# Moving the high and low parts of x by 224 bytes inside a partition

## The chip, the cores and the metric

The kernel runs on one core of one Trainium2 chip. The metric is the device time of the whole program in microseconds, median of the runs; lower is better. The profile beside it is one execution of the same program, with the start and the length of every instruction on every engine.

## The reference

Two layers of a decoder trunk over 256 tokens of width 1024 in float32. Layer 0 mixes tokens with stick-breaking attention, layer 1 with block-sparse attention, which over 256 tokens is plain causal softmax attention with rotary positions; each is followed by a squared-ReLU MLP of width 4096, and each of the four sub-layers closes with a layer norm over a scaled residual.

```python
    h = x
    for i in range(DEPTH):            # DEPTH = 2
        ln1_g, ln1_b, w1, w2, ln2_g, ln2_b = channel[i]
        h = layer_norm(DEEPNORM_ALPHA * h + mixers[i % N_MIXERS](h), ln1_g, ln1_b)
        h = layer_norm(DEEPNORM_ALPHA * h + squared_relu_mlp(h, w1, w2), ln2_g, ln2_b)
    return h
```

## The kernel before

Every large matmul is made of three: a float32 operand is split into a high part (rounded by a copy on ScalarE, L203) and a low part (the rest, a subtraction on VectorE, L204), and the product is high times high, high times low and low times high, added up in PSUM. `mm` (L189) issues one of them, `mm3` (L191) the three. In a matmul one operand, the stationary one, is loaded into the array as a block of 128x128, and the other, the moving one, streams past it. The trace names them in the order out<-moving,stationary.

The weights arrive as 64 "units" a layer of 1 MB, 512 rows by 512 columns, through SyncE's DMA queue into three raw buffers; ScalarE and VectorE split each into a `hi` and a `lo` tile, of which five pairs are live. The activations of a sub-layer's input stand transposed in two tiles for the whole program, `xh` and `xl` (eight blocks of 128 rows by 256 tokens each). Five loops read these:

- `projT` computes a transposed product: the stationary operand is a block of `hi` or `lo`, the moving one a row of `xh` or `xl` with 256 columns. It makes the queries and keys of layer 0 (`qkT_ps`) and the first MLP product (`up_ps`) of chunks 2 to 7 of both layers: the rows `qkT_ps<-xh,hi` and `up_ps<-xh,hi` and their two sisters each.
- `proj` computes tokens by columns: the stationary operand is a block of `xh` or `xl` (128 tokens), the moving one a row of `hi` or `lo` with 512 columns. It makes the values (`v_ps`) of both layers, the queries and keys (`qk_ps`) of layer 1 and the first two MLP chunks (`up_ps<-hi,xh`, from `up_tok`) of both layers.
- `down` (`dn_ps`) and `wo` (`wo_ps`) have the same shape as `proj`, with 512 moving columns of `hi` or `lo`, but their stationary blocks come from the tiles `hh`, `hl` (the MLP's hidden layer) and `oh`, `ol` (the attention's output).
- the scores (`sc`) multiply blocks of `qkh` and `qkl`, two heads beside each other on 64 partitions each; `o` multiplies the weights of the attention (`pt` moving) with the values (`v` stationary).
- transposes on TensorE (`xt`, `ht_ps`, `tp`, `pt_ps`) move the identity out of `const` past a stationary block of `h`, `r`, `qk` or `p`.

The order of all instructions is written out when the program is built: `Plan` holds a clock for each engine, with a fixed cost for each operation by its size, and issues what is due. Its costs know nothing of addresses. A norm (`norm`) is followed by `to_x`, which transposes the new `h` on TensorE and writes `xh` and `xl` again; the next `proj` waits for them.

The tiles stand in a partition in the order in which their pools are opened, each rounded up to 32 bytes. Where they begin, in bytes of the partition and modulo 512 (every block, row and buffer of a kind is a multiple of 512 bytes away from the first, but for the ten `t2k` and four `t3k` buffers):

| tile | first byte | modulo 512 |
|---|---|---|
| xh, xl | 2176, 10368 | 128 |
| h (2), v (2) | 18560, 26752 | 128 |
| const (identity) | 36000 | 160 |
| raw (3), hi (5), lo (5) | 50080, 74656, 115616 | 416 |
| qkh, qkl, r, qk, rot (ten t2k buffers) | 156576 | 416, 448, 480, 0, 32, ... 192 |
| p, keep (four t3k buffers) | 177376 | 224, 256, 288, 320 |
| pt (4) | 189792 | 352 |
| hh, oh (3), hl, ol (3) | 202080, 214368 | 352 |

Of the kernel before, what the change touches and what calls it, by code (L numbers as in the profile page):

```python
# [7 lines left out]
F32 = mybir.dt.float32  # L8
# [6 lines left out]
P = 128  # L15
# [11 lines left out]
SEQ = (("A0", "V0", "A1", "A2", "A3", "V1"), ("A0", "A1", "V0", "A2", "A3", "V1"))  # L27

RAWS, LIVE = 3, 5
N2K, N3K, NPT = 10, 4, 4  # L30
MARGIN, WINDOW = 0.5, 0.25
X_LOADS = {0: 1, 1: 1, 2: 2, 4: 2, 6: 2}
# [121 lines left out]
def trunk(ctx: ExitStack, tc: tile.TileContext, x, xt, cst, cstb, w, ln, out):  # L154
    nc = tc.nc

    def pool(name, bufs, **kw):
        return ctx.enter_context(tc.tile_pool(name=name, bufs=bufs, **kw))

    one = pool("one", 1)  # L160
# [39 lines left out]
    def split(n, hi, lo, src, after, rank=1, take=(), give=(), scale=None):  # L200
# [9 lines left out]
        b.first = a  # L210
        return b

    xh = one.tile([P, KT, T], F32R, tag="xh", name="xh")
    xl = one.tile([P, KT, T], F32R, tag="xl", name="xl")
    h = [one.tile([P, D], F32, tag=f"h{t}", name=f"h{t}") for t in range(NT)]
    v = [one.tile([P, D], F32, tag=f"v{t}", name=f"v{t}") for t in range(NT)]

    def tok(t):
        return slice(t * P, (t + 1) * P)
# [561 lines left out]
```

## Time and profile before

| | us |
|---|---|
| median of 3 runs | 613.29 (612.9 to 613.78) |
| the profiled execution, its own time | 613.18 |
| its span, from the first to the last instruction | 611.4 |
| TensorE busy in the span | 600.0 |
| VectorE, ScalarE, GpSimd busy | 389.4, 290.6, 24.6 |

Matmuls overlap: a record lasts from when a matmul starts to when its last result is out, and the next one starts long before that. So the busy time of TensorE says only that it never rests; what a matmul costs is the distance from its start to the next start. The chain of work that ended last gives it: it merges stretches of matmuls of one kind and writes their count and their time.

### The profile page before, as it was taken

What the parts mean: (1) busy time and instruction counts of PE and PEld (TensorE: products, weight loads), DVE (VectorE), ACT (ScalarE), POOL (GpSimd) and SP (SyncE); (2) the same over time, 40 slices, a digit from 0 to 9 for tenths busy, and PEclk for the clock granted to TensorE, in tenths of its full rate; (3) what the DMA queues carried; (4) which work ended last, traced back from release to release, by engine and by line L of the source; (5) the groups of instructions that cost most, each with busy time, mean ns of one, the idle gap of its engine ahead of it and who ended that gap; (6) DMA issues with size and microseconds to landing.
All of it is one profiled execution on the core that took longest, in us unless ns stands there. A gap on an engine that the chain in (4) does not pass through costs nothing.

```text
span 611.4 us, 8761 instructions
## 1 busy us (share of the span) xinstructions
PE 600.0 (98%) x3640; PEld 513.7 (84%) x3640; DVE 389.4 (64%) x489; ACT 290.6 (48%) x419; POOL 24.6 (4%) x30
## 2 busy tenths in 40 slices
PE   8999999999999999999999999999999999999994
PEld 6899987878899899898877777778798998898883
DVE  5787774777546445545779777768666437437444
ACT  5676663436444443543535655635356326335310
POOL 0000000000000000000032022000000000000000
PEclk9999999999999999999999999999999999999998
DMA  8984236175556346337175333332664374364201
GB/s 283 383 304 181 99 140 244 51 252 184 199 209 232 143 177 258 147 146 274 70 214 199 139 138 137 138 139 96 248 254 162 141 270 154 148 249 190 87 0 69
DMA packets 17751, 109.31 MB, mean 179 GB/s; under 512 B 1968, under 2 KB 2352, under 8 KB 5680
## 3 DMA queue, kind: packets, MB, share of 16 engines
q1 hardware_dynamic: 17712, 108.76, 48.6%
q8 instruction: 28, 0.46, 0.3%
q14 instruction: 11, 0.09, 0.0%
HBM read 107.71 MB, written 1.05 MB: 178 GB/s over the span
## 4 chain that ended last, share of the span: by engine, by line
PE 95%; DVE 2%; DMA 1%; ACT 1%; SPq 0%; issue 0%; DVEq 0%; ACTq 0%
PE dn_ps L189 29%; PE up_ps L189 29%; PE wo_ps L189 7%; PE v_ps L189 7%; PE qkT_ps L189 7%; PE qk_ps L189 7%; PE sc L189 3%; PE o L496 2%; DMA raw<-in_wqkv 1%; PE xt L373 1%; PE tp L543 1%; DVE lo L204 1%; DVE xl L204 1%; PE ht_ps L650 1%; PE pt_ps L478 1%; PE pt_ps L480 1%
## 5 line engine op out<-in xcount | busy, mean ns | idle before, releaser
L204 DVE TENSOR_TENSOR lo<-raw,hi 128x1024 fp32r<-128x1024 f32 (+1 forms) x196 | 229.8, 1213 | 47.8 <-ACT hi L203 46.0
L203 ACT CAST hi<-raw 128x1024 fp32r<-128x1024 f32 (+1 forms) x196 | 192.0, 1032 | 63.3 <-issue 42.4
L189 PE MATMUL up_ps<-xh,hi 128*128 128x256 f32 x384 | 108.1, 281 | 0.0
L189 PE MATMUL up_ps<-xl,hi 128*128 128x256 f32 x384 | 107.9, 281 | 0.0
L189 PE MATMUL up_ps<-xh,lo 128*128 128x256 f32 x384 | 107.8, 281 | 0.0
L189 PE MATMUL dn_ps<-hi,hl 128*128 128x512 f32 x256 | 100.8, 394 | 0.0
L189 PE MATMUL dn_ps<-lo,hh 128*128 128x512 f32 x256 | 100.2, 391 | 0.0
L189 PE MATMUL dn_ps<-hi,hh 128*128 128x512 f32 x256 | 99.7, 390 | 0.0
L617 DVE SCALAR_TENSOR_TENSOR r<-up_ps,r 128x512 f32<-128x512 f32 x32 | 22.0, 688 | 83.4 <-ACT r L615 83.4
L189 PEld LDWEIGHTS up_ps<-xl,hi 128*128 128x128 f32 x384 | 72.4, 188 | 0.5
L189 PEld LDWEIGHTS up_ps<-xh,hi 128*128 128x128 f32 x384 | 72.3, 188 | 0.5
L189 PEld LDWEIGHTS up_ps<-xh,lo 128*128 128x128 f32 x384 | 72.3, 188 | 0.0
L615 ACT ACTIVATE r<-up_ps 128x512 f32<-128x512 f32 x32 | 19.1, 596 | 100.5 <-PE up_ps L189 100.5
L189 PEld LDWEIGHTS dn_ps<-lo,hh 128*128 128x128 f32 x256 | 48.1, 188 | 10.6
L189 PEld LDWEIGHTS dn_ps<-hi,hh 128*128 128x128 f32 x256 | 48.1, 188 | 10.0
L189 PEld LDWEIGHTS dn_ps<-hi,hl 128*128 128x128 f32 x256 | 48.1, 188 | 9.8
L189 PE MATMUL qkT_ps<-xh,hi 128*128 128x256 f32 x128 | 37.6, 294 | 1.3 <-ACT hi L203 1.3
L189 PE MATMUL qkT_ps<-xh,lo 128*128 128x256 f32 x128 | 36.6, 286 | 0.2 <-DVE lo L204 0.2
L189 PE MATMUL qkT_ps<-xl,hi 128*128 128x256 f32 x128 | 36.4, 285 | 0.0
L203 ACT CAST xh<-xt 128x512 fp32r<-128x512 f32 x12 | 7.0, 587 | 42.9 <-PE xt L373 41.1
L189 PEld LDWEIGHTS qkT_ps<-xh,hi 128*128 128x128 f32 x128 | 24.6, 192 | 2.6 <-ACT hi L203 2.1
L189 PE MATMUL v_ps<-hi,xh 128*128 128x512 f32 x64 | 26.6, 416 | 0.0
(97 smaller groups left out, 889.2 us busy)
## 6 DMA issues: line engine op xcount, KB each, us to landing
raw<-in_w SPq DMA_DIRECT2D x64, 1024.0 KB, 5.0
raw<-in_wqkv SPq DMA_DIRECT2D x22, 1024.0 KB, 5.9
raw<-in_wo SPq DMA_DIRECT2D x8, 1024.0 KB, 4.7
raw<-in_wqkv SPq DMA_DIRECT2D x8, 256.0 KB, 6.5
gb<-in_l_ln_g SPq DMA_DIRECT2D x4, 512.0 KB, 3.7
gb<-in_l_ln_b SPq DMA_DIRECT2D x4, 512.0 KB, 5.2
h<-in_x SPq DMA_DIRECT2D x2, 512.0 KB, 6.7
out<-h SPq DMA_DIRECT2D x4, 256.0 KB, 2.1
```

The source lines that it names most:

```text
L189: nc.tensor.matmul(ps, sta, mov, start=start, stop=stop)
L203: f = lambda: nc.scalar.copy(hi(), src())
L204: g = lambda: nc.vector.tensor_tensor(lo(), src(), hi().bitcast(F32), op=ALU.subtract)
L373: nc.tensor.transpose(XB[t][:, n, k * P:(k + 1) * P], h[t][:, (4 * n + k) * P:(4 * n + k + 1) * P], ident)
L478: nc.tensor.transpose(ps[:, j, 0:P], pj[:, T:T + P], ident)
L480: nc.tensor.transpose(ps[:, j, T:T + P], pj[:, P:T], ident)
L496: nc.tensor.matmul(o[HD * j:HD * j + HD, 0, kt * P:T], v[kt][:, hd * HD:(hd + 1) * HD], pt[:, 0:T] if kt == 0 else pt[:, T:T + P], start=k ...
L543: nc.tensor.transpose(tb["tp"][:, pr, c0:c0 + P], QK[g, t]["qk"][:, e * T + pr * P:e * T + pr * P + P], ident)
L615: nc.scalar.activation(box["r", n], ps, AF.Relu)
L617: return dve(512, lambda: nc.vector.scalar_tensor_tensor(box["r", n], ps, 0.0, box["r", n], op0=ALU.max, op1=ALU.mult), after=[a], rank=0. ...
L650: nc.tensor.transpose(box["ht"][:, 0, k * P:(k + 1) * P], box["r", 0][:, k * P:(k + 1) * P], ident)
```

## The change

Two tiles that nothing reads or writes are put into the pool `one`: 224 bytes ahead of `xh` and 288 bytes behind `v`. `xh`, `xl`, the two `h` and the two `v` begin 224 bytes later, at 352 modulo 512 instead of 128. Everything behind them begins 512 bytes later, so that it keeps its place modulo 512. No instruction is added, removed or moved.

```diff
+GAP = (224, 288)
...
+    def shift(n):
+        one.tile([P, n // 4], F32, tag=f"gap{n}", name=f"gap{n}")
+
+    shift(GAP[0])
     xh = one.tile([P, KT, T], F32R, tag="xh", name="xh")
     xl = one.tile([P, KT, T], F32R, tag="xl", name="xl")
     h = [one.tile([P, D], F32, tag=f"h{t}", name=f"h{t}") for t in range(NT)]
     v = [one.tile([P, D], F32, tag=f"v{t}", name=f"v{t}") for t in range(NT)]
+    shift(GAP[1])
```

## Rows read from the trace of the kernel before

**Rows 1.** Page: span; each engine's busy time, share of the span, instructions
```profile
span 611.4 us, 8761 instructions
...
PE 600.0 (98%) x3640; PEld 513.7 (84%) x3640; DVE 389.4 (64%) x489; ACT 290.6 (48%) x419; POOL 24.6 (4%) x30
```

**Rows 2.** Page: chain that ended last, shares by engine, then by line
```profile
PE 95%; DVE 2%; DMA 1%; ACT 1%; SPq 0%; issue 0%; DVEq 0%; ACTq 0%
PE dn_ps L189 29%; PE up_ps L189 29%; PE wo_ps L189 7%; PE v_ps L189 7%; PE qkT_ps L189 7%; PE qk_ps L189 7%; PE sc L189 3%; PE o L496 2%; DMA raw<-in_wqkv 1%; PE xt L373 1%; PE tp L543 1%; DVE lo L204 1%; DVE xl L204 1%; PE ht_ps L650 1%; PE pt_ps L478 1%; PE pt_ps L480 1%
```

**Rows 3.** Waits of TensorE: for whom, us in total, times, longest
```profile
PE qkT_ps L189 <- ACT hi L203: 1.3, 1, 1.3
...
PE o L496 <- ACT pt L485: 0.2, 1, 0.2
```

**Rows 4.** Windows: stretch, its length, busy us of engines (instructions), clock, DMA
```profile
150.00:296.00 146.00, 146.00 (x903) 131.29 (x902) 80.35 (x86) 60.96 (x74) 0.99 (x1) 1.00 0.52 194
303.00:394.00 91.00, 90.76 (x513) 70.05 (x511) 72.19 (x124) 49.37 (x106) 16.29 (x9) 1.00 0.50 172
```

**Rows 5.** Groups of TensorE by form: count, busy us, mean ns, idle before
```profile
L189 PE MATMUL up_ps<-xh,hi 128*128 128x256 f32 x384 | 108.1, 281 | 0.0
...
L189 PE MATMUL dn_ps<-hi,hl 128*128 128x512 f32 x256 | 100.8, 394 | 0.0
...
L189 PE MATMUL qkT_ps<-xh,hi 128*128 128x256 f32 x128 | 37.6, 294 | 1.3 <-ACT hi L203 1.3
...
L189 PE MATMUL v_ps<-hi,xh 128*128 128x512 f32 x64 | 26.6, 416 | 0.0
```

**Rows 6.** Chain in order of time: start, us, what, count; undisturbed stretches
```profile
157.59 10.99 PE dn_ps L189 x48
168.58 11.36 PE up_ps L189 x96
...
303.37 6.29 PE qk_ps L189 x27
...
421.99 6.29 PE up_ps L189 x27
...
570.63 32.98 PE dn_ps L189 x144
```

**Rows 7.** Timeline of TensorE: first and last of the matmuls with x stationary
```profile
19.52 0.39 PE L189 MATMUL v_ps<-hi,xh 128*128 128x512 f32 x1
...
446.71 0.39 PE L189 MATMUL up_ps<-hi,xl 128*128 128x512 f32 x1
```

**Rows 8.** Chain in order of time: from the norm to layer 1's products
```profile
309.66 0.44 PE xt L373 x4
310.10 0.69 PE qk_ps L189 x3
310.79 0.66 PE xt L373 x4
311.47 0.59 ACT xh L203
312.09 1.29 DVE xl L204 x2
313.38 1.14 DVE lo L204
314.57 11.23 PE qk_ps L189 x47
```

**Rows 9.** Timeline of TensorE: one block of transposes of p
```profile
71.58 0.27 PE L478 MATMUL pt_ps<-const,p 128*128 128x128 f32 x1
...
72.13 0.27 PE L480 MATMUL pt_ps<-const,p 128*128 128x128 f32 x1
```

**Rows 10.** Timeline of TensorE: pairs of score matmuls, two blocks of 16
```profile
48.40 0.28 PE L189 MATMUL sc<-qkl,qkh 64*128 64x256 f32 x2
...
48.63 0.23 PE L189 MATMUL sc<-qkh 64*128 64x128 f32 x2
...
329.13 0.28 PE L189 MATMUL sc<-qkl,qkh 64*128 64x256 f32 x2
...
329.37 0.22 PE L189 MATMUL sc<-qkh 64*128 64x128 f32 x2
```

## The prediction

> **What bounds the kernel now.** The page comes first: TensorE is busy for 600.0 of 611.4 us, VectorE for 389.4 and ScalarE for 290.6 [rows 1]. Busy time of overlapping matmuls proves little, so the chain comes second: 95% of it is TensorE [rows 2], and nearly all of that the three-part products of `mm`, two shares of 29% for the MLP and four of 7% for the attention's projections. The waits come third: TensorE waits hardly at all once the first weights are there, 1.3 us for the first of them and 0.2 us at a single later place [rows 3]. The windows by stage come last: in the MLP of layer 0, and in the stage of layer 1 in which x is the stationary operand of almost everything, the granted clock is 1.00, the level of 2.4 GHz, and VectorE, the next busiest, is busy for 72.19 of 91 us [rows 4]. So the time is the sum of the distances from one matmul's start to the next, in a fixed order. A change that alters this distance alters the time; one that leaves it alone doesn't.
>
> **What a start costs, by operand.** The chain's stretches give the distance. With 512 moving columns and a stationary block of `hh` or `hl` (at 352 modulo 512), 48 matmuls take 10.99 us, 229.0 ns each, and 144 take 32.98, again 229.0 [rows 6]. With the same moving tiles, the same 512 columns and a stationary block of x (at 128), 27 take 6.29 us, 233.0 ns each, in layer 1's queries and in the MLP alike [rows 6]. All these run at the one clock, each in a steady rhythm. Shape, type, moving operand and PSUM use agree between the two kinds; what differs is the tile that the stationary block is read from. Whichever of the three buffers of `hh`, or of the five of `hi`, is in use, the rhythm stays, so large distances in a partition don't seem to matter, and the place modulo 512 is the difference that is left. With 256 moving columns of x (at 128) and a stationary block of `hi` or `lo` (at 416), 96 take 11.36 us, 118.3 ns each [rows 6].
>
> **The change part by part.** It adds and removes no instruction, and as the plan's costs know no address, the order stays.
>
> (a) x as stationary operand of `proj`. Nine groups of 64 have it, like the one shown: three parts each in `v_ps`, `qk_ps` and `up_ps` [rows 5], 576 matmuls between 19.52 and 446.71 us [rows 7]. Between these two rows 512 of the 576 are followed by the next start after 224 to 245 ns; the other 64 stand ahead of other work or of a wait and keep what they cost. With x at 352 and the weights still at 416, both places modulo 512 are those of `down`. So 512 x (233.0 - 229.0) = 2.05 us are saved. If the other 64 gain as well it is 576 x 4.0 = 2.30 us.
>
> (b) Of that, something is given back. At three places (before the second MLP chunk of either layer, and in layer 1's queries, the one shown) TensorE waits behind a norm: the second transposes of `xt`, then 0.59 us of ScalarE, 1.29 and 1.14 us of VectorE, then the products go on [rows 8]. The matmuls ahead of the transposes lie on the chain, but the 12 between these and the wait lie beside it: what they gain lengthens the wait. That is 3 x 12 x 4.0 ns = 0.15 us. What is late next there is VectorE's `lo`, and it is no later than now. Elsewhere VectorE has room: 72.19 of 91 us [rows 4] against a stage that shrinks by some 1.2 us (about 300 starts of 4.0 ns).
>
> (c) x as moving operand of `projT`: 1536 matmuls, three groups of 384 in the MLP and three of 128 in layer 0's queries and keys [rows 5]. They begin at 352 instead of 128, against weights at 416. No row has this pair of places. I take nothing. The nearest rows are the scores, which read q and k out of buffers at ten different places: their pairs with 256 columns start 0.23 us for two apart in one block and 0.24 in another [rows 10], 115 to 120 ns each, and no place stands out among the 16 blocks. They don't settle it: while a row of one buffer streams, the next block is loaded from the same buffer, so that the two places always agree modulo 512, and each covers 64 partitions. The bound: the one difference that a place makes in this trace is 4.0 ns for 512 columns, so 2.0 ns for 256 if it goes by columns and 4.0 if it goes by matmul, in either direction: 3.1 to 6.1 us saved or lost.
>
> (d) `h` and `v` move too. `h` is the stationary block of the 48 `xt` transposes; four take 0.44 us [rows 8], 110 ns each, from 128, and six of `p`, from 224 to 320 by block, run at the same pace: 0.55 us for five starts [rows 9]. So transposes don't feel the place; zero, bounded by 48 x 4.0 ns = 0.2 us either way. `v` is the stationary block of 128 matmuls of `o`; zero, bounded by 128 x 4.0 = 0.5 us. VectorE, ScalarE and the DMAs touch the same tiles with the same shapes; they stand on 4% of the chain [rows 2] and I take nothing.
>
> The sum: 2.05 - 0.15 = 1.90 us. The profiled execution took 613.18 us, 1.8 of it around the span, and lies 0.1 under the median of 613.29; 613.18 - 1.90 = 611.3 us.
>
> **The rivals.** (R1) The moving side answers too, and badly: x at 352 streams past weights at 416 with a stall that 128 doesn't have. Against it stands that the scores show no such case; for it, that a place does matter for the stationary side, and that nothing like this pair was ever run. From 1.90 / 1536 = 1.24 ns a matmul on the gain is eaten. At 2.0 ns it costs 3.1 us and gives 614.4 us, at 4.0 ns 6.1 and 617.4 us: slower than before.
>
> (R2) The moving side answers, and well: the difference of the two places, moving less stationary, is 64 in `down`, 288 in `proj` and 224 in `projT`; the change makes it 64 and -64. If it is nearness that helps, `projT` gains what `proj` does, 2.0 to 4.0 ns a matmul, and the time is 608.2 down to 605.2 us. For it: 118.3 ns is 11.6 over the 106.7 that 256 columns take at 2.4 GHz, so there is something to gain. Against it: the scores, in which the row that streams and the block that is loaded differ by 0, are no faster than `projT`.
>
> (R3) The place is not the cause, and the change doesn't do what it says: `xh` stays at 233.0 ns at any place, because of something else in which the tiles differ, and the time stays at 613.2 us. In favour, a rule of the Trainium skill speaks: its page "SBUF — State Buffer", section "Who interferes with whom", says that TensorE never waits on another reader of that memory, and "TensorE: Matmul & The Clock Gate", section "Step-by-step: what each phase is for", that loading the next weights takes no read bandwidth from the running matmul, since each has its port. By these two the place of a stationary block could not show, and the sum would be zero. Against R3: two steady rhythms, 229.0 and 233.0, that change with the stationary tile alone [rows 6].
>
> **How the numbers follow.** The forecast (a saving of 1.9, within half a microsecond) gets 0.60, R1 0.13, R2 0.12, R3 0.15. A measurement of this kernel can tell about 0.2%, 1.2 us, from no change. The forecast lies beyond it, but its lower end (0.15 us of waits, `v` and the 64 unsteady starts against it) comes near; I give 0.06 of its 0.60 to "same". R2 is faster; R3 is the same; R1 is half the same, at 614.4 and below, and half slower, with 0.03 more for a mishap in `o` or in the supply of weights. Faster: 0.54 + 0.12 = 0.66; same: 0.06 + 0.15 + 0.05 = 0.26; slower: 0.08. The range reaches from R2's nearer end, 608.2, to R1's, 614.4; the farther halves of both, some 0.13, are left out.
>
> **What would show it.** In the profile after: (a) is right if undisturbed stretches of `qk_ps` and of the early `up_ps` stand at 229 ns a start (27 in 6.18 us) and the means of the `proj` groups come down by some 4 ns; R3 if they stay at 6.29. (c) is right if 96 `up_ps` still take 11.36 us; R1 and R2 put them at 11.55 to 11.74 and at 11.17 to 10.98. (b) is right if the piece from the second `xt` to the products keeps its length. A different rhythm of `dn_ps` would make the whole reading wrong, since nothing of it is moved modulo 512.

## The result and the profile after

The changed kernel takes 605.87 us (median of six runs, 604.94 to 607.11), the kernel before 613.1 (six runs, 612.43 to 614.25): a ratio of 0.9876, 95% interval 0.9864 to 0.9888. That is 7.2 us less where 1.9 were forecast, and under the low end of the range, 608.2. The profiled execution of the changed kernel took 606.12 us, its span is 604.4.

The page of the changed kernel gives span and busy times, to set beside [rows 1]. Line numbers are higher by one near `mm` and by six farther down.

```profile
span 604.4 us, 8761 instructions
...
PE 592.5 (98%) x3640; PEld 508.3 (84%) x3640; DVE 389.5 (64%) x489; ACT 290.7 (48%) x419; POOL 24.6 (4%) x30
```

The same instructions; TensorE is busy for 7.5 us less, the other engines for as long as before. The chain of the changed kernel in order of time (start, us, what, count) shows where, beside [rows 6] and [rows 8]:

```profile
10.51 9.85 PE qkT_ps L190 x70
...
38.54 10.09 PE qkT_ps L190 x84
...
75.15 4.10 PE qkT_ps L190 x36
...
156.64 10.98 PE dn_ps L190 x48
167.62 10.91 PE up_ps L190 x96
...
300.15 6.18 PE qk_ps L190 x27
...
307.47 0.65 PE xt L379 x4
308.14 0.59 ACT xh L204
308.76 1.29 DVE xl L205 x2
310.05 1.14 DVE lo L205
311.24 11.03 PE qk_ps L190 x47
...
417.96 6.18 PE up_ps L190 x27
...
563.64 32.98 PE dn_ps L190 x144
```

Three readings. With x stationary, 27 starts take 6.18 us, 228.9 ns each instead of 233.0. `dn_ps`, whose places stay, keeps its 10.98 and 32.98 us. And with x moving, 96 starts take 10.91 us, 113.6 ns each instead of 118.3: a gain of 0.45 us in each of the twelve chunks of the two MLPs, 5.4 us in all, for which the forecast had nothing.

The chain of the kernel before gives the stretches of layer 0's queries and keys to compare:

```profile
11.14 8.54 PE qkT_ps L189 x70
...
38.11 10.14 PE qkT_ps L189 x84
...
75.19 4.26 PE qkT_ps L189 x36
```

From the end of the first stretch (19.68 us before, 20.36 after) to the end of the span it is 591.7 us before and 584.0 after, 7.7 us less: the 5.4 of the MLP, 1.6 of `proj` (all distances behind its 576 matmuls, added up from the timelines, are 140.7 us before and 139.1 after), and 0.7 of the queries and keys of layer 0. The 0.7 us that the span doesn't show went at the start: the first stretch began 0.63 us earlier than before and took 1.31 longer. This execution waited 1.7 us for the first weights, and the granted clock then fell to the lower level, 1.2 GHz, for 3 to 4 us, as the windows of the changed kernel show (stretch, length, busy us of PE, PEld, DVE, ACT and POOL with instructions, clock, DMA, GB/s):

```profile
11.00:13.00 2.00, 2.00 (x15) 2.00 (x14) 2.00 (x5) 1.88 (x5) 0.00 (x0) 0.69 1.11 433
13.00:15.00 2.00, 2.00 (x12) 2.00 (x11) 2.00 (x5) 1.40 (x3) 0.00 (x0) 0.50 0.97 403
15.00:17.00 2.00, 2.00 (x18) 2.00 (x18) 0.16 (x1) 0.69 (x1) 0.00 (x0) 0.96 1.04 414
```

The second stretch of the two chains, 84 starts, is the odd one: 10.14 us before, 10.09 after. At 113.6 ns it would have come down by 0.4 us. The same matmuls, with the same places, take 113.9 ns each in the 36 from 75.15 us on, and some 118 here. I come back to this.

### The profile page after: what moved, and what is told of

The parts are those of the page before. It is cut to its first block, busy times and chain, and to the rows that moved or that the text cites. A ratio compares the mean times of both kernels' runs of the same rounds, so it can differ in the third digit from the quotient of the medians.

```text
span 604.4 us, 8761 instructions
## 1 busy us (share of the span) xinstructions
PE 592.5 (98%) x3640; PEld 508.3 (84%) x3640; DVE 389.5 (64%) x489; ACT 290.7 (48%) x419; POOL 24.6 (4%) x30
## 4 chain that ended last, share of the span: by engine, by line
PE 95%; DVE 2%; DMA 1%; ACT 1%; SPq 0%; issue 0%; DVEq 0%; ACTq 0%
PE dn_ps L190 29%; PE up_ps L190 28%; PE wo_ps L190 7%; PE qkT_ps L190 7%; PE v_ps L190 7%; PE qk_ps L190 7%; PE sc L190 3%; PE o L502 2%; PE xt L379 1%; DMA raw<-in_wqkv 1%; PE tp L549 1%; DVE lo L205 1%; DVE xl L205 1%; PE ht_ps L656 1%; PE pt_ps L484 1%; PE pt_ps L486 1%
## 5 line engine op out<-in xcount | busy, mean ns | idle before, releaser
L190 PE MATMUL up_ps<-xh,hi 128*128 128x256 f32 x384 | 106.3, 277 | 0.0
L190 PE MATMUL up_ps<-xl,hi 128*128 128x256 f32 x384 | 106.1, 276 | 0.0
L190 PE MATMUL up_ps<-xh,lo 128*128 128x256 f32 x384 | 106.1, 276 | 0.0
```

The source lines that it names most:

```text
L190: nc.tensor.matmul(ps, sta, mov, start=start, stop=stop)
```

## The experiments

All compare stretches of the same order of instructions. "Moving less stationary" is the place of the moving operand less that of the stationary one; the expectations write it with its sign, the table below modulo 256. The times of runs without an interval are single ones; the kernel before took 612.1 to 613.6 us beside them, so the stretches of the chain carry the verdicts, not the times. In all these kernels the granted clock was 1.00, the level of 2.4 GHz, in the stretches compared.

**First four: what about the places counts.** Either x is put elsewhere, with all behind it at its old place modulo 512, or (w192) x stays and all behind `v` moves. `GAP` has four numbers from here on: the bytes ahead of `xh`, between `xh` and `xl`, behind `v`, and ahead of the hidden tiles; a zero puts no tile. The edits are shown against the kernel before, cut to the lines that differ, with the run's name as a comment.

```diff
+GAP = (256, 0, 256, 0)   # x384
+GAP = (32, 0, 480, 0)    # x160
+GAP = (288, 0, 224, 0)   # x416
+GAP = (0, 0, 288, 0)     # w192
```

> x begins at 384 modulo 512, weights stay at 416 and hidden tiles at 352: moving less stationary is -32 in projT and +32 in proj (the changed kernel has -64 and +64, the kernel before -288 and +288). Theory N (the two places have to be near each other modulo 512): as in the changed kernel or better, 96 up_ps in at most 10.9 us (113.6 ns each), 27 qk_ps in at most 6.18 us. Theory M (the difference has to be a multiple of 64): slow again, 11.36 and 6.29 us. Theory A (both places have to be at 32 modulo 64, as 352 and 416 are): 384 is not, so slow, 11.36 and 6.29 us.

> x begins at 160 modulo 512: moving less stationary is -256 in projT and +256 in proj, the farthest there is. N: slow, 96 up_ps in 11.36 us and 27 qk_ps in 6.29 us, as before the change. M (256 is a multiple of 64) and A (160 is at 32 modulo 64): fast, 10.91 and 6.18 us.

> x stays where it was before the change (128); all that stands behind v is moved by 288 bytes, weights to 192, hidden tiles to 128 modulo 512. Differences are those of the changed kernel (-64 in projT, +64 in proj and down), the places themselves are not. N and M (only the difference counts): 96 up_ps in 10.91 us, 27 qk_ps in 6.18, 48 dn_ps in 10.99. A (the places count, and none is at 32 modulo 64 now): 11.36, 6.29, and dn_ps slower than 10.99 as well.

> x begins at 416 modulo 512, as the weights do: difference 0 in projT and proj. N: fast, if nearness is what helps it is the best place, under 10.91 us for 96 up_ps and under 6.18 for 27 qk_ps. M and A: as in the changed kernel, 10.91 and 6.18 us. If the two places must differ so that the two readers don't meet, slow: 11.36 and 6.29.

w192, chain:

```profile
155.03 10.98 PE dn_ps L190 x48
166.02 10.91 PE up_ps L190 x96
...
298.54 6.18 PE qk_ps L190 x27
```

x384, chain:

```profile
168.44 11.36 PE up_ps L190 x96
...
303.23 6.29 PE qk_ps L190 x27
```

x160, chain:

```profile
168.43 11.52 PE up_ps L190 x96
...
304.02 6.14 PE qk_ps L190 x27
```

x416, chain:

```profile
167.46 11.52 PE up_ps L190 x96
...
303.06 6.14 PE qk_ps L190 x27
```

w192 (604.62 us) has the changed kernel's stretches to the hundredth with x where it was, so theory A falls: the difference of the two places counts, not either place. x384 stands nearer to the weights than the changed kernel and is as slow as before (613.01 us), x416 has a difference of 0 and is slower still with x moving: theory N, nearness, falls. x160 refutes M: 256 is a multiple of 64, and `projT` is slow. And differences that are 256 apart agree: 0 and 256 (x416, x160: 11.52 and 6.14), 224 and 480 (the kernel before and x384: 11.36 and 6.29). x160 also takes the change apart: `proj` gains even more than in the changed kernel, `projT` loses, and the whole takes 613.33 us, as before.

**The next eight: the map of the differences.** Those at 16 modulo 32 read x from 16 bytes behind a tile's first byte, `xl` like `xh`, as the tiles themselves are rounded up to 32.

```diff
+GAP = (96, 0, 416, 0)    # x224
+GAP = (480, 0, 32, 0)    # x96
+GAP = (192, 0, 320, 0)   # x320
+GAP = (160, 0, 352, 0)   # x288
+GAP = (288, 480, 192, 0) # x432
+GAP = (320, 480, 160, 0) # x464
+GAP = (352, 480, 128, 0) # x496
+GAP = (224, 480, 256, 0) # x368
...
-    xh = one.tile([P, KT, T], F32R, tag="xh", name="xh")
+    xh = one.tile([P, KT * T + 8], F32R, tag="xh", name="xh")[:, 4:4 + KT * T].rearrange("p (k q) -> p k q", q=T)
```

> x at 224 modulo 512, weights at 416: moving less stationary is -192 in projT and +192 in proj, which is 64 modulo 128 as in the changed kernel, and three times as far. Theory D128 (only the difference modulo 128 counts): the same as the changed kernel, up_ps at 114.0 ns a start (96 in 10.9 us), qk_ps at 229 (27 in 6.18). Rival D512 (64 itself is the good distance, of all that there are): as slow as at 256 or 288, 118 to 120 ns and 228.5 to 233 ns.

> x at 432: +16 in projT, -16 (112 modulo 128) in proj; the two tiles are read from 16 bytes behind their first byte, nothing else differs. If the difference counts in steps of 32 bytes, each rate is one of those of the neighbours: 119.9 (0) or that of 32 in projT, 118.3's partner or 228.6 in proj. If it counts in smaller steps, they are new values.

> x at 464: +48 in projT, -48 (80 modulo 128) in proj. In steps of 32: projT as at 64 (114.0) or at 32 (not measured yet); proj as at 64 (229) or at 96. If the stall falls gradually towards 64: projT between 114 and 118.

> x at 496: +80 in projT, -80 (48 modulo 128) in proj. In steps of 32: projT as at 64 (114.0) or at 96 (118.3); proj as at 32 (233.0) or at 64 (229). If one of the two lies under 114 or under 228 ns, there is a better place than the one of the change.

> x at 96, weights at 416: moving less stationary is -320 in projT, 320 in proj. Modulo 256 that is 192 and 64, as in the changed kernel. Theory D256 (the difference counts modulo 256; so far 0 and 256 agree, and 224 and 480): as the changed kernel, up_ps at 114.0 ns a start (96 in 10.9 us), qk_ps at 229, the whole within 603 to 607 us. Rival (one place or one distance alone is good, each other is some shade of slow): 117.8 to 120 ns and 612 us or more.

> x at 320: -96 in projT (160 modulo 256), +96 in proj. D256 has no value for either yet. If the good range lies around 192 in projT (64 in proj), 160 is fast too, at most 115 ns; if 192 alone is good, 117.8 to 120 ns.

> x at 288: -128 in projT, +128 in proj, both 128 modulo 256, the farthest from 0 under D256. If the stall comes where the two readers meet (0: 119.9 ns), 128 is the best place in projT: under 114 ns a start and under 606 us. If 192 alone is good: 117.8 to 120 ns, 612 us or more.

> x at 368: -48 in projT (208 modulo 256), +48 in proj. Between the 114.0 ns of 192 and the 118.3 ns of 224: gradual means about 116 ns, steps of 32 mean 114 ns. In proj 48 lies between 229 ns (64) and 233 ns (32).

x224, chain:

```profile
168.29 11.30 PE up_ps L190 x96
...
302.86 6.30 PE qk_ps L190 x27
```

x96, chain:

```profile
167.69 10.91 PE up_ps L190 x96
...
300.22 6.18 PE qk_ps L190 x27
```

x224 refutes D128: its difference agrees with the changed kernel's modulo 128, its stretches don't. x96 bears out D256: its difference is 256 away from the changed kernel's, and its stretches are the same again (606.21 us). What the rest gave, with two more kernels of below, from the same two stretches of each chain:

| x at | moving less stationary in `projT`, modulo 256 | 96 up_ps, us | 27 qk_ps, us | one time, us |
|---|---|---|---|---|
| 416, 160 | 0 | 11.52, 11.52 | 6.14, 6.14 | 612.35, 613.33 |
| 432 | 16 | 11.39 | 6.31 | 614.55 |
| 448 | 32 | 11.20 | 6.30 | 610.96 |
| 464 | 48 | 11.36 | 6.29 | 612.9 |
| 224 | 64 | 11.30 | 6.30 | 612.53 |
| 496 | 80 | 11.52 | 6.27 | 617.52 |
| 0 | 96 | 11.51 | 6.33 | 617.21 |
| 288 | 128 | 11.52 | 6.30 | 616.32 |
| 320 | 160 | 11.39 | 6.29 | 615.19 |
| 352 (changed), 96, w192 | 192 | 10.91, 10.91, 10.91 | 6.18, 6.18, 6.18 | 604.62 to 606.21 |
| 368 | 208 | 11.44 | 6.30 | 614.6 |
| 128 (before), 384 | 224 | 11.36, 11.36 | 6.29, 6.29 | 612.08 to 613.56 |

There is no slope towards 192 (208, 16 bytes away, is slower than 224), no steps of 32, and no worst place where two readers meet: 0, 80, 96 and 128 are equally slow. Of the twelve differences tried one is good for `projT`, and the eleven others reach from 116.7 to 120.0 ns a start. In `proj`, where the difference has the other sign, two are good: 27 starts take 6.14 us at 0, 6.18 at 64, and 6.27 to 6.33 at the ten others.

Stretches of `projT` with other work ahead of them bear this out in part: the 75 `up_ps` behind the last `ht_ps` take 8.52 us at 192 and 8.75 to 9.00 elsewhere, the 36 `qkT_ps` 4.10 and 4.21 to 4.31. The order of the slow ones changes (at 128 the 75 run at 118.7 ns a start, not 120.0), and the 84 `qkT_ps` gain nothing at 192: 10.09 us there, 10.05 to 10.27 elsewhere.

The times in the last column hold more than these stretches. In x0, x288, x320 and x432 the granted clock fell at the start of the program, as in the changed kernel's profile: the first 70 starts took 9.85 to 10.14 us. In x496 `down` was slower, as shown below.

**One part alone, and whose place counts.** xl128 moves `xh` alone (the second unused tile stands between `xh` and `xl`, which puts `xl`, `h` and `v` back to 128); lo448 moves the low parts of the weights alone, by 32 bytes. x448 and x0 are the two last places in steps of 32.

```diff
+GAP = (224, 288, 0, 0)   # xl128
+GAP = (224, 0, 288, 0)   # lo448
+GAP = (320, 0, 192, 0)   # x448
+GAP = (384, 0, 128, 0)   # x0
...
     splits = pool("splits", LIVE)
+    gl = pool("gl", 1)
+    gl.tile([P, 8], F32, tag="gl", name="gl")
+    lows = pool("lows", LIVE)
+    gr = pool("gr", 1)
+    gr.tile([P, 120], F32, tag="gr", name="gr")
...
-                            self.lo = splits.tile([P, 4, 512], F32R, tag="lo", name=f"lo{i}")
+                            self.lo = lows.tile([P, 4, 512], F32R, tag="lo", name=f"lo{i}")
```

The lines below the first cut are those of lo448 alone.

> One part of the change alone: xh begins at 352, xl (and h and v) stay at 128 modulo 512. If each matmul answers to its own operands, two of the three kinds of projT (xh,hi and xh,lo) run at 114 ns and xl,hi at 118.3, 115.5 ns in the mean and about 608 us; in proj hi,xl at 233 and the two with xh at 229. If the rhythm of the triple as a whole has to fit, all three are slow: 118 ns, 612 us or more.

> The changed kernel with the low parts of the weights alone moved by 32 bytes, to 448; hi stays at 416, x at 352. Low parts are the stationary operand of xh,lo in projT; they are loaded while xl,hi streams, and used while the next hi is loaded. Theory L (a stream is slowed by the block that is loaded beside it): xl,hi slow (118.6 ns, the rate measured at a difference of 160), xh,hi and xh,lo at 114. Theory U (by the block that it streams past): xh,lo slow, the other two at 114. Theory T (the rhythm of the three as a whole): all three at 116 to 120. In down the moving lo stands 96 from the stationary block (233.2 ns by proj at 96) and hi 64 (229).

> x at 448: +32 in projT, -32 (224 modulo 256) in proj, one of the two places in steps of 32 without a value. By D256, 192 in projT is the only place so far with 114 ns; if it is alone, 118 to 120 ns here, 612 us or more. If fewer bits count and 32 is good as well, 114 ns and 605 us.

> x at 0 modulo 512: -416 in projT (96 modulo 256), +416 (160 modulo 256) in proj, the other place in steps of 32 without a value. If 192 in projT is alone: 118 to 120 ns, 612 us or more; if good places lie 96 apart (192 less 96), 114 ns.

The groups by form give the mean length of a record (last number before the bar's end); the changed kernel:

```profile
L190 PE MATMUL up_ps<-xh,hi 128*128 128x256 f32 x384 | 106.3, 277 | 0.0
L190 PE MATMUL up_ps<-xl,hi 128*128 128x256 f32 x384 | 106.1, 276 | 0.0
L190 PE MATMUL up_ps<-xh,lo 128*128 128x256 f32 x384 | 106.1, 276 | 0.0
```

xl128, the same groups:

```profile
L190 PE MATMUL up_ps<-xl,hi 128*128 128x256 f32 x384 | 108.7, 283 | 0.0
L190 PE MATMUL up_ps<-xh,hi 128*128 128x256 f32 x384 | 108.4, 282 | 0.0
L190 PE MATMUL up_ps<-xh,lo 128*128 128x256 f32 x384 | 107.1, 279 | 0.0
```

lo448, the same groups:

```profile
L195 PE MATMUL up_ps<-xh,lo 128*128 128x256 f32 x384 | 109.5, 285 | 0.0
L195 PE MATMUL up_ps<-xl,hi 128*128 128x256 f32 x384 | 108.6, 283 | 0.0
L195 PE MATMUL up_ps<-xh,hi 128*128 128x256 f32 x384 | 108.2, 282 | 0.0
```

lo448, chain:

```profile
168.63 11.39 PE up_ps L195 x96
...
191.17 11.73 PE up_ps L195 x96
```

In both, the kind whose own operand stands at an odd place is the longest, but all three are longer than in the changed kernel, though two of them have its places. The distances to the next start, averaged from the timelines over the ten stretches of 96, say it more plainly: behind xh,hi, xl,hi and xh,lo they are 113.8, 113.6 and 113.4 ns in the changed kernel, 119.1, 121.7 and 115.4 in xl128, and 118.0, 118.7 and 123.7 in lo448. 96 starts take 11.41 us in xl128 (615.9 us in all) and, by turns from chunk to chunk, 11.39 and 11.73 in lo448 (616.73). L would have slowed xl,hi alone in lo448 and U xh,lo alone; neither did. Of the three theories T, the rhythm of the three as a whole, is left, with the odd one carrying most of it; a rule by single pairs in which a late start also delays its neighbours was not tried against it. Two of the three kinds at the good difference are worth nothing in these two kernels: 96 starts take no less than before the change. Of the 3.8 us by which xl128 is slower than the kernel before it was run with, some 3.1 lie in `down`, as the next part shows.

**What is carried over.** The chains of x496 and xl128 show more. In both the weights and the hidden tiles stand 64 apart, as in the kernel before and in the changed one. x496:

```profile
157.18 11.20 PE dn_ps L190 x48
168.38 11.52 PE up_ps L190 x96
...
299.86 5.51 PE dn_ps L190 x24
```

xl128:

```profile
157.21 11.00 PE dn_ps L190 x48
168.21 11.41 PE up_ps L190 x96
179.62 11.20 PE dn_ps L190 x48
...
459.78 11.20 PE dn_ps L190 x48
```

`down` runs at 233.3 ns a start in one stretch (11.20 us for 48) and at 229.2 to 229.6 in another of the same kernel, with nothing of its own changed. In x496 the longer distance follows upon `up_ps`, and the 24 starts behind the transposes of a norm have the shorter. So a pair of places allows more than one rhythm. That the one that a stretch keeps depends on how it is entered fits this, but what decides it is not shown: in xl128 both the `down` at 157.21 us and its twin in layer 1, at 459.78, follow 75 starts of `up_ps`, and they differ. The odd stretch of the changed kernel shows two rhythms too: 84 starts at about 118 ns, and 36 at 113.9, of one kind at one pair of places.

The last two kernels were timed four times each. w192t is w192 again; w192s moves the hidden tiles of `down` and `wo` by another 64 bytes, to a difference of 0 (with them only the norms' small tiles, which stand behind).

```diff
+GAP = (0, 0, 288, 0)     # w192t
+GAP = (0, 0, 288, 64)    # w192s
...
+    gst = pool("gst", 1)
+    gst.tile([P, GAP[3] // 4], F32, tag="gap3", name="gap3")
     st = pool("st", 3)
```

The last lines are those of w192s alone.

> The kernel of w192 again, timed: x where it was before the change, all behind v moved by 288 bytes, so that only the differences are those of the changed kernel. If the differences alone make the gain: a ratio to the kernel before of 0.985 to 0.990, as the changed kernel's 0.9876. If x itself had to be moved: 0.998 to 1.002.

> As w192t, with the hidden tiles of down and wo moved by another 64 bytes to 192, so that moving less stationary is 0 there. proj at 0 ran at 228.5 ns a start, down now runs at 229.0: if down takes proj's value, 960 starts save 0.5 us, 0.1% under w192t, which this many rounds can hardly tell; if the rhythm of projT is upset by what runs ahead of it, its 96 up_ps leave 10.91 us and the whole is 2 to 5 us slower than w192t.

w192t: 605.99 us against 613.26, ratio 0.9883 (0.9861 to 0.9905), the changed kernel's gain with x unmoved. Its first stretches had the full clock, its chain the same stretches:

```profile
155.63 10.99 PE dn_ps L190 x48
166.62 10.91 PE up_ps L190 x96
...
299.16 6.18 PE qk_ps L190 x27
```

w192s: 607.85 us, ratio 0.991 (0.9887 to 0.9932):

```profile
146.49 8.51 PE up_ps L192 x75
155.00 10.89 PE dn_ps L192 x48
165.90 11.31 PE up_ps L192 x96
...
299.74 6.19 PE qk_ps L192 x27
```

`down` gained more than expected, 226.9 instead of 229.0 ns a start; the value of `proj` at 0 by x416's chain is 227.4, not the 228.5 of the expectation. But `up_ps`, of which nothing was moved, went from 10.91 to 11.31 us for 96 starts, 117.8 ns each, which is the rate that x224 shows at another difference. In the same kernel the 75 starts of `up_ps` ahead of the first `down` still take 8.51 us, 113.5 ns each, so its places alone don't make `projT` slow here: it is slow where `down` with its new rhythm runs ahead. (That the writes to the moved hidden tiles disturb it is a rival that no run took apart.) The gain of 0.1 us in each `down` stretch costs 0.4 us in the next `up_ps`, and the whole is 1.9 us slower than w192t by the medians; the two intervals overlap, and the stretches carry the difference. w192, at 604.62 us once and 605.99 in w192t, is as fast as the changed kernel; none of the study is clearly faster.

## Why the prediction was wrong

(a) was right in its price: 6.18 us for 27 starts with x stationary was the number that it named, and came. Of its 2.05 us 1.6 arrived: the long stretches come down to 228.9 ns a start, the short ones between two interruptions to about 230. (b) was right: from the second transposes of `xt` to the products behind the norm it is 3.78 us before (310.79 to 314.57) and 3.77 after (307.47 to 311.24). (d) was right: four `xt` take 0.44 us in both chains, and the distances behind the 128 matmuls of `o`, added up from the timelines, are 12.26 us in both.

The step that failed is (c), the zero for x as moving operand. It stands for 1536 of the kernel's 3640 matmuls and gave 6.1 of the 7.7 us: 5.4 in the MLPs, where each start gave 4.7 ns, over the bound of 4.0 that the step set, and 0.7 in layer 0's queries and keys. Its ground was the scores, among which no buffer stood out. They couldn't carry it, for two reasons. The prediction says that their two places always agree modulo 512; that holds for the row that streams and the block that is loaded next. By the measure of the experiments, moving less stationary of one matmul, it holds for one pair in three: in `sc<-qkl,qkh` and `sc<-qkh,qkl` row and block lie in different buffers. And each pair of matmuls has only one distance in a block: behind the second and the third pair, with 256 columns, these are 112 to 122 ns in the 16 blocks, and single distances scatter as far (115 to 123) inside the 84 steady starts of `qkT_ps` in the kernel before. So a difference of 4.7 ns could not stand out there. The prediction itself said that the scores don't settle it, and still the zero was taken and given 0.60.

R2 named the right operand, and its bounds, 608.2 to 605.2 us, hold the 605.87 that was measured. That it landed inside is partly luck: an MLP start gained more than the 4.0 ns of its upper bound, the 288 starts of layer 0 that can be compared only 2.4 each, and (a) gave less than forecast. Its reason, that the two places come near each other, is wrong: 32 apart (x384) and 0 apart (x416) are slow, and 192 apart counted the other way (x96) is fast. It held more than the chance of 0.12, since the same rows that made (a) credible, a rate that changes with nothing but a place, spoke for any stream of the same kind, `projT` among them. R1 didn't happen here. That x can stream more slowly than before is shown by x416 and x160, with 120.0 ns a start instead of 118.3, but this is under R1's lower price of 2.0 ns: it adds 1.8 us in the MLPs, and as `proj` gains in both they end at 612.35 and 613.33 us. The 616 to 618 us of x0, x288 and x496 hold the low clock at the start or, in x496, 3.2 us more in `down`. R3 is refuted by w192t, x96 and the changed kernel itself. By the rule of the Trainium skill that the prediction named with it ("SBUF — State Buffer", section "Who interferes with whom": TensorE never waits on another reader), read as the prediction read it, the place could not have shown in any of these kernels. It did, with 113.6 to 120.0 ns a start, so here the measurement decides. What the rule says of other engines was not tried; these runs moved only TensorE's own two operands against each other, and what they touch with them.

The prediction's last sign, that another rhythm of `dn_ps` would upset the reading, did come, not in the changed kernel but in x496 and xl128. So the reading "the place modulo 512 is the difference that is left" was too simple in two ways: it is the difference of two places, modulo 256 as far as tried, and the rhythm of what runs ahead takes part.

Why one difference lets three matmuls of 256 columns run at 113.6 ns and another not, these runs don't say. That the loading of the next block and the running stream get in each other's way is a guess that no run shows: lo448, made to separate the block that is loaded from the one in use, showed neither alone.

## What to carry to other kernels

Where TensorE is the bound and its records follow each other without a wait, the distance from start to start belongs in the profile's reading for each kind of operand pair, beside the other pairs with as many columns: 7 us of 613 lay in it here. It can be moved by padding tiles, at no instruction's cost, but by trial and not by rule: measure several differences of moving and stationary place, read the stretches of every stage, as the rhythm of one stage can change that of the next, and repeat it after anything that moves a tile. When a rate is found to depend on something, the zero for the most frequent kind that shares it needs a row of its own.

## What the runs showed of the hardware

- In the long stretches of the MLPs and of `proj`, at a granted clock of 1.00, the distance between starts depends on moving less stationary place in a partition, modulo 256 in all three pairs tried (0 and 256, 224 and 480, 192 and 448). With 256 columns (`up_ps` of `projT`) it is 113.6 ns at 192 and 116.7 to 120.0 at the eleven others; with 512 columns and x stationary it is 227.4 at 0, 228.9 at 64 and 232.2 to 234.4 at the ten others.
- Sixteen bytes matter: 96 `up_ps` take 10.91 us at 192 and 11.44 at 208.
- One pair of places can carry two steady rhythms: `down` at 229.2 or 233.3 ns a start within xl128, `up_ps` at 113.5 or 117.8 within w192s, `qkT_ps` at 113.9 or near 118 within the changed kernel.
- At the start of the program the granted clock fell to the level of 1.2 GHz behind a wait of 1.7 us in the changed kernel's profile and stayed at 2.4 GHz behind one of 1.3 us in the kernel before; the first 70 matmuls behind it took 9.85 and 8.54 us. The length of the wait alone doesn't decide it: x320 and x224 both waited 2.0 us at the same place, and from 11 to 13 us the clock was 0.52 in x320 (10.09 us for the 70) and 1.00 in x224 (8.51).
